# Experts of an MoE layer: gathering four experts at once and scattering in float32r parts, gates on the down product, a shorter ring

## The chip, the cores and the metric

The kernel runs on one core of a Trainium2 chip. Times are device microseconds (us) of that core. The time before is the median of three runs; the profile is of one further execution. In the text PE is TensorE, DVE VectorE, ACT ScalarE, POOL GpSimd, and SP the engine on whose queue the weights are loaded.

## The reference, cut to what matters

The reference is one layer over 256 latent tokens of width 2048: modulations, one input projection, retention and attention heads, an output projection, a norm, a hierarchical mixture of experts, a second norm. The change lies in the mixture:

```python
g_onehot = one_hot(argmax(g_logits), 4)                  # 1 of 4 groups
top_v, top_i = top_k(e_logits_of_the_group, 2)           # 2 of its 8 experts
top_w = softmax(top_v) * g_prob
for gi in range(4):                                      # 32 experts, D = 2048, hidden 512
    hid = silu(t @ w_gate[gi]) * (t @ w_up[gi])
    y = y + (hid * gate[gi]) @ w_down[gi]
```

Here t is the token after the first norm, with a shift and a scale. All arithmetic is in 32-bit floats.

## The kernel before, in words

The 32 experts are taken as 16 pairs, counted here from 0 (loop at L1093). Each expert has room for 64 tokens, so that a pair fills 128 rows. An expert's weights are 12 chunks of 1 MB, 8 for gate and up and 4 for down: 384 chunks, which SP loads in order (`stream`, L141) into a ring of 15 tiles (9 of the pool `ring`, 4 of `st`, 2 of `sa`). `expert_chunk` (L967) starts the load of the chunk 14 places ahead; the load waits until its tile is free. Two of the first chunks go to tiles that are used for other things later (`early_chunks`, L977).

For a pair the work is: one-hot matrices `oh` of which token sits in which row (L1097); the gather, `gather_some`, a product of the normalised tokens `nn` with `oh` in float32, 32 products of 128x128 in four PSUM banks, evacuated with scale and shift to `xg` by DVE (L997) and ACT (L994) in turn; gate and up of the first expert, `gate_up`, 32 products (L1013), then silu on ACT (L1016), a product on DVE (L1017), two transposes (L168) and a copy to `hT` on ACT (L1022); the down product of the first expert, four blocks of 512 columns, each 8 products (L1031) and two DVE products with modulation 5 into `Dm` (L1035); gate and up of the second expert; and then four steps, one for each block of 512 columns: the down product of the second expert and the scatter, a float32 product of `Dm` with `sT` (L1041), which DVE adds to the residual `h` (L1042). `sT` is the transpose of the one-hots times the gates, `go` (L1114). Where a row of the profile counts float32 products of PE it counts two passes for each, so 8 products of the down step stand as x16.

A scheduler places the instructions of each engine in order. PE, DVE and ACT each work through theirs one after the other, so that what waits holds up all that stands behind it on that engine. After pair 4 the kernel reads from memory whether an expert has more than 64 tokens and branches (`overflow`, L1046); it has not, so the branch leads past the loop. In the first `gate_up` of pair 15 the weights of the second norm are brought to all partitions by PE (`norm2_weights`, L1086) and ACT (L1088). Before pair 0, `nn` is made by POOL (L900) for the first 128 tokens and by ACT (L898) for the others, while DVE does the router.

Of the kernel before, what the change touches and what calls it, by code (L numbers as in the profile page):

```python
# [10 lines left out]
F32 = mybir.dt.float32  # L11
# [14 lines left out]
LOOKAHEAD = 14  # L26
EARLY = (7, 14)
# [41 lines left out]
# columns of the small weights  # L69
# [51 lines left out]
def tile_kernel(ctx: ExitStack, tc, a, out):  # L121
# [28 lines left out]
    # ---------------------------------------------------------------- constants  # L150
# [26 lines left out]
    def affine(eng, hp, mean, rstd, wt, b, nbias):  # L177
        """Normalise, scale and shift, on VectorE or on GpSimd."""
# [22 lines left out]
    # ------------------------------------------------- modulations 2..5, rows of w_ada on VectorE  # L201
# [74 lines left out]
    def matmul3(p, l, rr, first=True, last=True):  # L276
        """Product of operands in two parts each, without the product of the two small ones."""
# [4 lines left out]
    # ---------------------------------------------------------------- retention heads  # L282
# [25 lines left out]
    def ret_setup():  # L308
# [23 lines left out]
        # powers of the decay for the context: column (tile, direction, head)  # L332
# [11 lines left out]
    def ret_tables(h):  # L344
        """Decay between latent tokens (a diagonal tile and both off it), and from the context."""
# [12 lines left out]
    def ret_head(h):  # L358
# [4 lines left out]
        # state left by the context, both directions  # L363
# [35 lines left out]
    def ret_norm(h0):  # L399
        """Normalise four heads."""  # L400
# [29 lines left out]
    def mla_latents():  # L430
        # normalised latents, transposed in place
# [30 lines left out]
        # rotary keys, on both halves of the partitions  # L462
# [8 lines left out]
    # ---------------------------------------------------------------- phase A  # L471
# [170 lines left out]
    with tc.tile_pool(name="ml", bufs=1) as ml, tc.tile_pool(name="ml2", bufs=2) as ml2:  # L642
        cqT, kvT, kpT = mla["cqT"], mla["kvT"], mla["kpT"]
        # rotary queries
# [8 lines left out]
        # latents in two parts; rotary keys and queries with the parts one above the other  # L653
# [23 lines left out]
        def up(g):  # L677
            """Keys, values and queries of two heads."""
# [81 lines left out]
    # ---------------------------------------------------------------- output projection, first norm  # L760
    ring = ctx.enter_context(tc.tile_pool(name="ring", bufs=9))
# [43 lines left out]
    def router_part(n, half):  # L805
        """Two blocks of 128 columns, transposed into what is no longer needed of modulation 2."""
# [76 lines left out]
    # ---------------------------------------------------------------- router  # L883
    nnp = ctx.enter_context(tc.tile_pool(name="nnp", bufs=1, side="right"))
    nn = nnp.tile([128, 2, D], F32)
    ro = ctx.enter_context(tc.tile_pool(name="ro", bufs=1))
    # 1 / deviation and -mean / deviation
    for t in range(2):
        for j, (c0, c1) in enumerate(((CUT, D), (0, CUT))):
            A.activation(nn[:, t, c0:c1], h[:, t, c0:c1], AF.Square, bias=hs[:, t, 2:3],  # L890
                         accum_out=hs[:, t, 4 + j:5 + j])
# [5 lines left out]
        if t:  # L897
            A.activation(nn[:, t], h[:, t], AF.Identity, bias=hs[:, t, 5:6], scale=hs[:, t, 4:5])  # L898
        else:
            G.tensor_scalar(nn[:, t], h[:, t], hs[:, t, 4:5], hs[:, t, 5:6], op0=OP.mult, op1=OP.add)  # L900
# [21 lines left out]
    # one more than the rank of a token among those of the same expert, 0 where it is not sent there  # L922
# [8 lines left out]
    def router_weights():  # L931
        # weights of the chosen two
# [29 lines left out]
    order = [i for i in range(last + 8) if i not in EARLY] + list(range(last + 12, last + 20))  # L962
    for n in range(4):
        order += [last + 8 + n, last + 20 + n]
    fetched, early = {}, {}

    def expert_chunk(i):  # L967
        if i in early:
            return early.pop(i)
        pos = order.index(i)  # L970
        while len(fetched) <= min(pos + LOOKAHEAD, len(order) - 1):
            j = len(fetched)
            pool = (st, sa, ring)[(j % 15 >= 4) + (j % 15 >= 6)]
# [3 lines left out]
    def early_chunks():  # L977
        """Two of the first chunks, in tiles that have another use later."""
        for i, name in zip(EARLY, ("Dm", "xg")):
            t = mo.tile([128, D], F32, name=name, **({"bufs": 1} if name == "Dm" else {}))  # L980
            SP.dma_start(t, dram2(a["wexp"], i * 128 * D, 128, D))
            early[i] = t

    def gather_some(xg, k4, oh, width):
        p = bankT()
        for j in range(4):
            for t in range(2):
                T.matmul(p[:, 128 * j:128 * j + width], nn[:, t, 128 * (k4 + j):128 * (k4 + j) + 128],  # L988
                         oh[:, t, :width], start=(t == 0), stop=(t == 1))
        for j in range(4):  # L990
            k = k4 + j
            src = p[:, 128 * j:128 * j + width]
            if j % 2:
# [6 lines left out]
    def new_xg():  # L1000
        return mo.tile([128, D], F32, name="xg").rearrange("p (k n) -> p k n", k=KB)

    def gate_up(xg, c0, src, before=None):
        """Hidden values of up to 64 tokens, transposed."""
# [12 lines left out]
        V.tensor_tensor(hid, pg[:, 256:512], hid, op=OP.mult)  # L1017
        pt = bankT()
# [6 lines left out]
    def down(hT, src, Dm, half, n):  # L1025
# [7 lines left out]
        for cg in range(2):  # L1033
            sl = slice(512 * n + 256 * cg, 512 * n + 256 * cg + 256)
            V.tensor_tensor(Dm[rows, sl], pd[64 * cg:64 * cg + 64, :256], mod5[rows, sl], op=OP.mult)  # L1035

    def scatter(Dm, sT, K, n):
        sl = slice(512 * n, 512 * n + 512)
        for t in range(2):
            p = bankA()  # L1040
            T.matmul(p, sT[:K, t, :], Dm[:K, sl], start=True, stop=True)  # L1041
            V.tensor_tensor(h[:, t, sl], p, h[:, t, sl], op=OP.add)  # L1042

    def overflow():
        v = nc.values_load(flag[0:1, 0:1], min_val=0, max_val=256)
        with tc.If(v > CAP):  # L1046
            with tc.For_i(0, E, 1) as e:
                with tc.For_i(1, S // CAP, 1) as c:
                    rc = mo.tile([128, 2, 1], F32, name="rc", bufs=1)
                    gc = mo.tile([128, 2, 1], F32, name="gc", bufs=1)  # L1050
                    V.tensor_copy(rc, rk[:, :, ds(e, 1)])
                    V.tensor_copy(gc, gt[:, :, ds(e, 1)])
                    io = mo.tile([128, 64], F32, name="io", bufs=1)
                    V.tensor_copy(io, C("iota")[:, ds(c * CAP + 1, CAP)])
                    oh = mo.tile([128, 2, 64], F32, name="ohf", bufs=1)
                    go = mo.tile([128, 2, 64], F32, name="gof", bufs=1)
# [162 lines left out]
```

## Time and profile before

| | |
|---|---|
| three runs | 1730.43, 1731.16, 1734.97 us; median 1731.16 us |
| span of the profiled execution | 1728.5 us |
| PE busy | 1595.0 us (92% of the span) |
| DVE busy | 860.4 us (50%) |
| ACT busy | 381.5 us (22%) |
| POOL busy | 115.2 us (7%) |
| first product of pair 0 to the end of the span | 718.97 to 1728.5 us |

The profiled execution has no time of its own beside its span, which lies 2.7 us under the median of the three runs. The median counts what lies around the span too.

How to read it: a busy PE of 92% says little, since the matmuls overlap. What counts in the expert stage is the distance from one pair to the next (60.34 us for most pairs), what PE does in it one after the other, and whether the loads keep pace with it.

### The profile page before, as it was taken

The page shows a single profiled execution, that of the slowest core. Times are in us where ns is not written, and L with a number is a line of the kernel's source. Part 1 is how long each engine was busy: PE and PEld are TensorE (multiplying, and loading weights), DVE is VectorE, ACT ScalarE, POOL GpSimd, SP SyncE. Part 2 cuts the span into 40 slices and gives each one's busy share as a digit, 9 for nine tenths or more (in the row PEclk, how much of TensorE's full clock was granted, in tenths as well). Part 3 has the DMA queues.
Part 4 walks back from the last instruction along what each step waited for, and adds up shares of the span by engine and source line. Part 5 has one row for each costly group of instructions (what it writes and reads, how often), then busy time and mean ns, then how long its engine had stood idle before and what let it go on. Part 6 is the DMA issues. An engine that isn't in the chain of part 4 may idle for free. (4 is left out here: it accounts for less than half of the span.)

```text
span 1728.5 us, 21531 instructions
## 1 busy us (share of the span) xinstructions
PE 1595.0 (92%) x8730; PEld 958.4 (55%) x8730; DVE 860.4 (50%) x1563; ACT 381.5 (22%) x710; POOL 115.2 (7%) x94
## 2 busy tenths in 40 slices
PE   5999999987889899599999979999999999999995
PEld 4667686866868777344454434554444454444442
DVE  6877685798798777622331321332323233232306
ACT  3323232334665433410100000110010011001010
POOL 1000000074322100200000000000000000000001
PEclk8999999999999999799999999999999999999998
DMA  7787777756554589798999998999999999999981
GB/s 317 282 330 284 304 305 282 271 206 225 187 195 168 227 301 360 297 368 347 417 419 417 417 376 332 409 420 419 415 418 420 416 418 419 418 416 417 419 303 49
DMA packets 81591, 579.36 MB, mean 335 GB/s; under 512 B 9360, under 2 KB 9808, under 8 KB 11856
## 3 DMA queue, kind: packets, MB, share of 16 engines
q1 hardware_dynamic: 81360, 577.91, 83.8%
q8 instruction: 70, 1.15, 0.3%
q14 instruction: 33, 0.27, 0.0%
q0 software_dynamic: 128, 0.03, 0.0%
HBM read 575.81 MB, written 2.10 MB: 334 GB/s over the span
## 5 line engine op out<-in xcount | busy, mean ns | idle before, releaser
L1013 PE MATMUL pA<-st,xg 128*64 128x512 f32 x2032 | 447.5, 593 | 0.1
L1013 PEld LDWEIGHTS pA<-st,xg 128*64 128x64 f32 x2032 | 144.3, 137 | 273.0 <-issue 255.1
L1031 PE MATMUL pA<-st,hT 128*64 128x256 f32 x2048 | 238.5, 383 | 4.6 <-ACT hT L1022 4.6
L1017 DVE TENSOR_TENSOR hid<-pA,hid 128x256 f32<-128x256 f32 x32 | 13.6, 425 | 420.1 <-ACT hid L1016 420.1
L1031 PEld LDWEIGHTS pA<-st,hT 128*64 128x64 f32 x2048 | 140.0, 137 | 109.1 <-issue 26.9
L584 PE MATMUL pA<-wlo,xhi 128*128 128x512 f32 (+1 forms) x480 | 188.1, 392 | 10.3 <-DVE wlo L263 10.2
L583 PE MATMUL pA<-whi,xhi 128*128 128x512 f32 (+1 forms) x480 | 185.4, 394 | 3.4 <-ACT whi L262 3.3
L262 ACT CAST whi<-st 128x1024 fp32r<-128x1024 f32 (+3 forms) x130 | 124.7, 962 | 287.0 <-PE pA L585 175.0
L1035 DVE TENSOR_TENSOR Dm<-pA,ada_acc 64x256 f32<-64x256 f32 x256 | 108.1, 422 | 160.7 <-PE pA L1031 158.3
L585 PE MATMUL pA<-whi,xlo 128*128 128x512 f32 (+1 forms) x480 | 185.8, 387 | 0.0
L239 DVE SCALAR_TENSOR_TENSOR ada_acc<-st,c,ada_acc 128x1024 f32<-128x1024 f32 x128 | 176.8, 1401 | 11.2 <-DMA st<-in_ada_dram 11.0
L263 DVE TENSOR_TENSOR wlo<-st,whi 128x1024 fp32r<-128x1024 f32 (+2 forms) x122 | 134.7, 1112 | 56.0 <-ACT whi L262 55.4
L988 PEld LDWEIGHTS pT<-oh,nn 128*128 128x128 f32 x1024 | 125.6, 196 | 38.8 <-issue 38.0
L988 PE MATMUL pT<-oh,nn 128*128 128x128 f32 x1024 | 138.5, 286 | 7.1 <-PEq L1046 5.5
L994 ACT ACTIVATE xg<-pT,modt 128x128 f32<-128x128 f32 x128 | 58.4, 458 | 332.9 <-DVE xg L997 328.7
L1041 PE MATMUL pA<-Dm,sT 128*128 128x512 f32 x256 | 121.2, 596 | 4.9 <-DVE Dm L1035 4.9
L1016 ACT ACTIVATE hid<-pA 128x256 f32<-128x256 f32 x32 | 12.3, 384 | 497.2 <-PE pA L1013 497.2
L1042 DVE TENSOR_TENSOR h<-pA,h 128x512 f32<-128x512 f32 x128 | 88.3, 690 | 57.2 <-PE pA L1041 57.2
L583 PEld LDWEIGHTS pA<-whi,xhi 128*128 128x128 f32 x480 | 90.5, 191 | 37.6 <-ACT whi L262 17.9
L584 PEld LDWEIGHTS pA<-wlo,xhi 128*128 128x128 f32 x480 | 91.8, 191 | 32.2 <-DVE wlo L263 14.5
L585 PEld LDWEIGHTS pA<-whi,xlo 128*128 128x128 f32 x480 | 92.0, 192 | 16.3
L997 DVE TENSOR_SCALAR xg<-pT,modt 128x128 f32<-128x128 f32 x128 | 52.1, 408 | 50.8 <-PE pT L988 23.1
(342 smaller groups left out, 1462.2 us busy)
## 6 DMA issues: line engine op xcount, KB each, us to landing
st<-in_wexp_dram SPq DMA_DIRECT2D x382, 1024.0 KB, 12.3
st<-in_ada_dram SPq DMA_DIRECT2D x96, 1024.0 KB, 6.8
st<-in_win_dram SPq DMA_DIRECT2D x35, 1024.0 KB, 6.8
st<-in_wo_dram SPq DMA_DIRECT2D x16, 1024.0 KB, 5.0
st<-in_wuq_dram SPq DMA_DIRECT2D x3, 1024.0 KB, 4.8
xn<-in_x_dram SPq DMA_DIRECT2D x2, 1024.0 KB, 6.5
xn<-in_ctx_dram SPq DMA_DIRECT2D x2, 1024.0 KB, 17.0
st<-in_wukv_dram SPq DMA_DIRECT2D x2, 1024.0 KB, 5.0
```

Of the source, the lines that this page charges most:

```text
L239: V.scalar_tensor_tensor(accs[m][:, sl], w[:, sl], c2[:, k, 0:1], accs[m][:, sl], op0=OP.mult, op1=OP.add)
L262: A.copy(hi, src)
L263: (eng or V).tensor_tensor(lo, src, hi, op=OP.subtract)
L583: T.matmul(banks[t][:, :wd], xh[:, sl], hi[:, kk, :wd], start=fst, stop=False)
L584: T.matmul(banks[t][:, :wd], xh[:, sl], lo[:, kk, :wd], start=False, stop=False)
L585: T.matmul(banks[t][:, :wd], xl[:, sl], hi[:, kk, :wd], start=False, stop=lst)
L988: T.matmul(p[:, 128 * j:128 * j + width], nn[:, t, 128 * (k4 + j):128 * (k4 + j) + 128], oh[:, t, :width], start=(t == 0), stop=(t == 1))
L1013: T.matmul(pg[64 * cg:64 * cg + 64], xg[:, k, c0:c0 + 64], c[:, kk, 512 * cg:512 * cg + 512], start=(k == 0), stop=(k == KB - 1))
L1031: T.matmul(pd[64 * cg:64 * cg + 64, :256], hT[:, f % 2, 64 * (f // 2):64 * (f // 2) + 64], c[:, f, 256 * cg:256 * cg + 256], start=(f == 0 ...
L1035: V.tensor_tensor(Dm[rows, sl], pd[64 * cg:64 * cg + 64, :256], mod5[rows, sl], op=OP.mult)
L1041: T.matmul(p, sT[:K, t, :], Dm[:K, sl], start=True, stop=True)
L1042: V.tensor_tensor(h[:, t, sl], p, h[:, t, sl], op=OP.add)
```

## The change

The chunk list, the number of experts in a pair and the products of gate, up and down stay. What changes:

- The gather is for four experts at a time, 256 rows, in float32r: `nn` is split into a high and a low part (a cast on ACT, L262, and a subtraction on DVE, L263), and each of the 16 blocks takes four products of 128x256. The tile `xg` is now 16 KB wide a partition and has one buffer. The plain `nn` is made by DVE alone, in four pieces.
- `gather_all` for the next four experts stands after the second `gate_up` of every odd pair, and behind the overflow branch for experts 24 to 27.
- The gates no longer stand in the one-hots: `back` makes a column of gates, `gcol`, and the DVE instruction of the down product multiplies by it as well. The transposed one-hots `sT` are float32r.
- The scatter splits `Dm` into a high and a low part, again by ACT and DVE, and takes four float32r products of 128x512 instead of two float32 ones.
- The ring pool has 6 tiles, 12 in all, the load runs 11 chunks ahead, and no chunk is loaded early elsewhere.
- The overflow branch stands after pair 5. The weights of the second norm have their own tile.

```diff
-LOOKAHEAD = 14
-EARLY = (7, 14)
+RING = 6
+LOOKAHEAD = 5 + RING
...
-            A.activation(nn[:, t], h[:, t], AF.Identity, bias=hs[:, t, 5:6], scale=hs[:, t, 4:5])
-            G.tensor_scalar(nn[:, t], h[:, t], hs[:, t, 4:5], hs[:, t, 5:6], op0=OP.mult, op1=OP.add)
+        for c0 in (0, D // 2):
+            cs = slice(c0, c0 + D // 2)
+            V.tensor_scalar(nnf[t][:, cs], h[:, t, cs], hs[:, t, 4:5], hs[:, t, 5:6], op0=OP.mult, op1=OP.add)
+            hi_lo(nnh[0][:, t, cs], nnh[1][:, t, cs], nnf[t][:, cs])
...
+    def new_xg():
+        return mo.tile([128, KB, 256], F32, name="xg", bufs=1)
+    def gather_two(xg, k2, oh, width):
+        p = bankT()
+        for j in range(2):
+            for i in range(4):
+                T.matmul(p[:, 256 * j:256 * j + width], nnh[i % 2][:, i // 2, ks], oh[:, i // 2, :width],
+                         start=(i == 0), stop=(i == 3))
...
-            V.tensor_tensor(Dm[rows, sl], pd[64 * cg:64 * cg + 64, :256], mod5[rows, sl], op=OP.mult)
+            V.scalar_tensor_tensor(Dm[rows, sl], pd[64 * cg:64 * cg + 64, :256], gcol[rows, half:half + 1],
+                                   mod5[rows, sl], op0=OP.mult, op1=OP.mult)
...
     def scatter(Dm, sT, K, n):
         sl = slice(512 * n, 512 * n + 512)
+        hl = [mo.tile([128, 512], F32R, name=f"D{j}") for j in range(2)]
+        hi_lo(hl[0][:K], hl[1][:K], Dm[:K, sl])
         for t in range(2):
             p = bankA()
-            T.matmul(p, sT[:K, t, :], Dm[:K, sl], start=True, stop=True)
+            for j in range(2):
+                T.matmul(p, sT[:K, t, :], hl[j][:K], start=(j == 0), stop=(j == 1))
             V.tensor_tensor(h[:, t, sl], p, h[:, t, sl], op=OP.add)
...
+            hid = gate_up(xg, 128 * pq + 64, src[1])
+            if pq and not final and q != 2:
+                xg = gather_all(q + 1, lambda: hT.append(flip_hid(hid)))
+            else:
+                hT.append(flip_hid(hid))
...
-        if pr == 4:
-            overflow()
+            if pr == 5:
+                overflow()
+                xg = gather_all(q + 1)
```

Where the instructions come to stand shows the order in which the scheduler left them. First PE in the four steps at the end of a pair, before (pair 3; L1031 is the down product, L988 the gather of the next pair, L1041 the scatter):

```order
L168 MATMUL pT<-ct,hid 128x128 x2
L988 MATMUL pT<-oh,nn 128x128 x3
L1031 MATMUL pA<-st,hT 64x256 x8
L988 MATMUL pT<-oh,nn 128x128 x5
L1041 MATMUL pA<-Dm,sT 128x512 x2
L1031 MATMUL pA<-st,hT 64x256 x8
L988 MATMUL pT<-oh,nn 128x128 x5
L1041 MATMUL pA<-Dm,sT 128x512 x2
```

and now, in pair 4, which has no gather (L1053 is the down product, L1067 the scatter; D_7217 is the high part of a block and D_7218 its low part, D_7242 and D_7243 those of the next block):

```order
L1053 MATMUL pA<-st,hT 64x256 x8
L1042 MATMUL pT<-gt,oh 128x2 x2
L1067 MATMUL pA<-D_7217,sT 128x512 x2
L1053 MATMUL pA<-st,hT 64x256
L1067 MATMUL pA<-D_7218,sT 128x512 x2
L1053 MATMUL pA<-st,hT 64x256 x7
L1067 MATMUL pA<-D_7242,sT 128x512 x2
L1053 MATMUL pA<-st,hT 64x256
L1067 MATMUL pA<-D_7243,sT 128x512 x2
```

The five gather products that stood between a down product and its scatter are gone, and between the products of the high and of the low part stands one product of the next block.

Next PE behind the second `gate_up` of pair 3, which now holds the gather of experts 8 to 11 (L991; a number behind a name tells buffers apart, so pT_6231 to pT_6264 are four of the eight banks' worth of results; 8 products go to each):

```order
L991 MATMUL pT_6231<-oh_6172,nn0_5490 128x256
...
L1053 MATMUL pA_6277<-st_6081,hT_6218 64x256
L991 MATMUL pT_6242<-oh_6172,nn0_5490 128x256
...
L991 MATMUL pT_6253<-oh_6172,nn0_5490 128x256
...
L1053 MATMUL pA_6277<-st_6081,hT_6218 64x256 x2
L991 MATMUL pT_6264<-oh_6172,nn0_5490 128x256
...
L1053 MATMUL pA_6277<-st_6081,hT_6218 64x256 x5
L168 MATMUL pT_6427<-ct_69,oh_6172 128x128 x2
L1042 MATMUL pT_6432<-gt_4698,oh_6172 128x2 x2
L1067 MATMUL pA_6292<-D0_6288,sT_6055 128x512
```

Six of the eight banks' worth now stand between the second `gate_up` and the first scatter, in and around the first down product; two more stand ahead of that `gate_up`.

Last DVE in the router, just ahead of pair 0 (`nnf` is the plain `nn`, nn_5491 its low part, `sel` the choice of experts, L916 to L926 the router's steps):

```order
L903 TENSOR_SCALAR nnf<-h,hs 128x1024
L263 TENSOR_TENSOR nn_5491<-nnf,nn_5490 128x1024 x3
L903 TENSOR_SCALAR nnf<-h,hs 128x1024
L917 MAX_INDEX gi<-gm,L 128x8
L916 MAX gm<-L 128x8
L941 TENSOR_SCALAR w<-gm 128x1
L918 CAST gf<-gi 128x8
```

All four L903 and all four L263 stand ahead of `sel`; none of them was on DVE before.

## Rows read from the trace of the kernel before

**Rows 1.** Windows: start:end, length, busy (instructions) by engine; clock; DMA share, GB/s.

```profile
1163.64:1223.98 60.34, 58.15 (x343) 28.54 (x343) 17.95 (x44) 5.18 (x12) 0.00 (x0) 1.00 1.01 419
968.35:1038.27 69.92, 56.68 (x311) 26.28 (x310) 16.69 (x40) 3.80 (x9) 0.00 (x0) 0.98 0.94 386
1038.27:1103.31 65.04, 62.92 (x376) 32.36 (x375) 19.54 (x47) 6.55 (x15) 0.00 (x0) 1.00 0.89 366
1646.32:1728.50 82.18, 62.60 (x343) 28.74 (x342) 31.69 (x55) 10.86 (x20) 5.87 (x4) 0.91 0.44 164
```

**Rows 2.** SP's waits: us in total, times, longest.

```profile
SPq L141 <- PE pA L1013: 421.6, 236, 21.1
```

**Rows 3.** Chain of waits in pair 7: start, us, what.

```profile
1202.41 1.88 PE pA L1031 x16
1204.29 1.31 PE pT L988 x10
1205.60 1.72 PE pA L1041 x4
...
1222.04 2.01 PE pT L988 x18
```

**Rows 4.** Timeline, a step of pair 4: start, us, engine, what, idle before.

```profile
1006.96 1.95 PE L1031 MATMUL pA<-st,hT 128*64 128x256 f32 x16 [0.52 <-ACT hT L1022]
...
1008.95 0.86 DVE L1035 TENSOR_TENSOR Dm<-pA,ada_acc 64x256 f32<-64x256 f32 x2 [3.00 <-PE pA L1031]
...
1009.86 1.98 PE L1041 MATMUL pA<-Dm,sT 128*128 128x512 f32 x4 [0.96 <-DVE Dm L1035]
...
1011.78 1.95 PE L1031 MATMUL pA<-st,hT 128*64 128x256 f32 x16
```

**Rows 5.** Groups of instructions: busy us, mean ns of one, idle before.

```profile
L262 ACT CAST whi<-st 128x512 fp32r<-128x512 f32 x18 | 11.1, 619 | 14.1 <-PE pA L585 14.1
L263 DVE TENSOR_TENSOR wlo<-st,whi 128x512 fp32r<-128x512 f32 x18 | 11.8, 676 | 2.0 <-ACT whi L262 1.9
L428 DVE SCALAR_TENSOR_TENSOR mix<-pT,sm,mix 128x256 fp32r<-128x256 f32 x8 | 3.5, 471 | 0.2 <-ACT mix L427 0.2
L545 ACT ACTIVATE xf<-pT,modc 128x256 f32<-128x256 f32 x32 | 16.4, 561 | 6.0 <-DVE modc L526 3.2 <-DVE xlo L547 2.5 <-PE pT L168 0.4
L1041 PE MATMUL pA<-Dm,sT 128*128 128x512 f32 x256 | 121.2, 596 | 4.9 <-DVE Dm L1035 4.9
L988 PE MATMUL pT<-oh,nn 128*128 128x128 f32 x1024 | 138.5, 286 | 7.1 <-PEq L1046 5.5 <-issue 1.1 <-DVE oh L1097 0.5
L263 DVE TENSOR_TENSOR wlo<-st,whi 128x1024 fp32r<-128x1024 f32 x95 | 116.2, 1229 | 53.9 <-ACT whi L262 53.5
L199 DVE TENSOR_SCALAR xn<-xn,bnm,bnr 128x2048 f32<-128x2048 f32 x4 | 5.3, 1334 | 0.0
```

**Rows 6.** Timeline, float32r products of 128x512, then of 128x256.

```profile
585.42 0.39 PE L834 MATMUL pA<-whi,mix 128*128 128x512 f32 x1
585.65 0.39 PE L835 MATMUL pA<-wlo,mix 128*128 128x512 f32 x1
...
503.70 0.28 PE L278 MATMUL pA<-whi,kv 128*128 128x256 f32 x1
503.82 0.28 PE L279 MATMUL pA<-cq,whi 128*128 128x256 f32 x1
```

**Rows 7.** Timeline, the start of the expert stage.

```profile
707.05 1.91 DVE L896 SCALAR_TENSOR_TENSOR L<-L,hs,rc 128x40 f32<-128x40 f32 x1
...
715.60 1.86 DVE L1114 TENSOR_SCALAR go<-ct,rk,gt 128x64 f32<-128x64 f32 x8
...
718.97 7.09 PE L1013 MATMUL pA<-st,xg 128*64 128x512 f32 x32
```

**Rows 8.** Timeline, behind the branch, and norm weights in pair 15.

```profile
1031.87 4.20 PE L988 MATMUL pT<-oh,nn 128*128 128x128 f32 x23 [5.49 <-PEq L1046]
...
1650.27 1.16 PE L1086 MATMUL pT<-ct,sm 128*128 128x128 f32 x8
```

More of the change, by code (lines that the diff above doesn't have):

```diff
@@ L961, in tile_kernel @@
     last = (E - 2) * 12
-    order = [i for i in range(last + 8) if i not in EARLY] + list(range(last + 12, last + 20))
+    order = list(range(last + 8)) + list(range(last + 12, last + 20))
     for n in range(4):
         order += [last + 8 + n, last + 20 + n]
-    fetched, early = {}, {}
+    fetched = {}
     def expert_chunk(i):
-        if i in early:
-            return early.pop(i)
         pos = order.index(i)
@@ L1017, in gate_up, with flip_hid @@
         V.tensor_tensor(hid, pg[:, 256:512], hid, op=OP.mult)
+        return hid
+    def flip_hid(hid):
         pt = bankT()
@@ L1023, in gate_up, with places, back, down @@
         return hT
-    def down(hT, src, Dm, half, n):
+    def places(oh, rank, c0, width, first):
+        for t in range(2):
+            V.tensor_scalar(oh[:, t, c0:c0 + width], first, rank[:, t], None, op0=OP.is_equal)
+    def back(oh, gates, width):
+        p = bankT()
+        for t in range(2):
+            transpose(p[:width, 128 * t:128 * t + 128], oh[:, t].bitcast(F32))
+        sT = mo.tile([128, 2, 128], F32R, name="sT")
+        V.tensor_copy(sT[:width].rearrange("p t n -> p (t n)"), p[:width, :256])
+        q = bankT()
+        for t in range(2):
+            T.matmul(q[:width, 0:2], oh[:, t].bitcast(F32), gates[:, t], start=(t == 0), stop=(t == 1))
+        gcol = mo.tile([128, 2], F32, name="gcol")
+        V.tensor_copy(gcol[:width], q[:width, 0:2])
+        return sT, gcol
+    def down(hT, src, Dm, gcol, half, n):
         rows = slice(64 * half, 64 * half + 64)
@@ L1140, in tile_kernel, with new_places, gather_all @@
-    lnw, lnb = nn[:, 0], nn[:, 1]
+    def new_places(q):
+        oh = mo.tile([128, 2, 256], F32R, name="oh")
+        for s in range(4):
+            places(oh, rk[:, :, 4 * q + s:4 * q + s + 1], 64 * s, 64, C("iota")[:, 1:65])
+        return oh
+    def gather_all(q, between=None):
+        ohs[q] = new_places(q)
+        xg = new_xg()
+        for k2 in range(0, KB, 2):
+            gather_two(xg, k2, ohs[q], 256)
+            if between and k2 == 4:
+                between()
+        return xg
@@ new lines, in tile_kernel @@
+    ohs = {0: new_places(0)}
+    xg = new_xg()
+    for q in range(E // 4):
+        for pq in range(2):
+            pr = 2 * q + pq
+            final = pr == E // 2 - 1
+            src = [lambda j, e=2 * pr + s: expert_chunk(e * 12 + j) for s in range(2)]
+            if final:
+                nns.close()
+                lnwb = ctx.enter_context(tc.tile_pool(name="lnp", bufs=1, side="right")).tile([128, 2, D], F32, name="lnwb")
+            if pr:
+                hid = gate_up(xg, 128 * pq, src[0], norm2_weights if final else None)
+            else:
+                hid = gate_up(xg, 0, src[0], lambda kc: gather_two(xg, 2 * kc, ohs[0], 256))
+                router_weights()
+                ada_finish(5)
+            sT, gcol = back(ohs[q][:, :, 128 * pq:128 * pq + 128], gt[:, :, 2 * pr:2 * pr + 2], 128)
+            hT = [flip_hid(hid)]
+            Dm = new_Dm()
+            if not final:
+                for n in range(4):
+                    down(hT[0], src[0], Dm, gcol, 0, n)
+            hid = gate_up(xg, 128 * pq + 64, src[1])
+            if pq and not final and q != 2:
+                xg = gather_all(q + 1, lambda: hT.append(flip_hid(hid)))
+            else:
+                hT.append(flip_hid(hid))
+            for n in range(5):
+                if n < 4 and final:
+                    down(hT[0], src[0], Dm, gcol, 0, n)
+                if n:
+                    scatter(Dm, sT, 128, n - 1)
+                    if final:
+                        for t in range(2):
+                            V.bn_stats(st2[:, t, n - 1], h[:, t, 512 * n - 512:512 * n])
+                if n < 4:
+                    down(hT[1], src[1], Dm, gcol, 1, n)
+            if pr == 5:
+                overflow()
+                xg = gather_all(q + 1)
```

119 lines of the change are left out of this document (33 added, 86 removed).

## The prediction

> **What bounds the kernel now.** I read the windows first, one from each pair's first gate product to the next one's, because the expert stage is most of the span and its pairs repeat. Twelve of the pairs 1 to 14 take 60.34 us like the one shown, with PE at full clock and the DMA share at 1.01, 419 GB/s [rows 1]. A pair is 24 chunks of 1,048,576 bytes; at 419 GB/s that is 60.1 us. So two things are nearly level: PE's program of a pair, 60.34, and the loads, 60.1. The reader is to see that shortening PE's program alone can give back at most 0.3 us a pair, but lengthening it costs in full. Pairs 4 and 5, on either side of the branch, are 69.92 and 65.04, together 14.3 over two ordinary ones, with the DMA share down to 0.94 and 0.89 [rows 1]: there the loads lose time as well. Then the queue's waits: SP waits mostly for the gate products to free tiles [rows 2], so a tile that PE frees late starts a load late.
>
> Third, the chain of waits inside a pair: nearly all of it is PE. A step at its end is down 1.88, gather 1.31, scatter 1.72, 4.91 from step to step, and behind the last scatter stand 2.01 of gather [rows 3]. Fourth, the timeline of pair 4, which has no gather in its steps: PE ends the down product at 1008.91, idles 0.96 for the two DVE products (0.86) that make `Dm`, and comes to the next down product 4.82 after this one began [rows 4]. So in other pairs the gather in a step fills a wait that would be there anyway: 1.31 of PE work costs 0.09. That is the key to the change.
>
> **Part by part.** The sum is made against the profiled span, 1728.5, which lies 2.7 below the median.
>
> *PE's own work.* The scatter has 256 float32 passes [rows 5], 0.43 apart (1.72 for four, rows 3); it gets 256 float32r products of 128x512 at 0.23 (585.42 to 585.65) [rows 6]: about 52 us less. The gather has 1024 passes [rows 5], 0.112 apart (2.01 for 18, rows 3), and gets 512 at 0.12 [rows 6]: some 55 less. What matters is what waits are bared.
>
> *A step.* The first scatter product now needs the high part. Behind the last down product come two DVE products, 0.86 [rows 4] (0.94 by the nearest instruction with a scalar and two operands, 471 ns, rows 5; I take 0.9), the cast on ACT, 0.62 [rows 5], and handovers of some 0.1: PE waits 1.6, where nothing stands in front of it to fill the time. Then two products of the high part, 0.45, one of the next down product, 0.23, beside which DVE subtracts (0.68, rows 5), two of the low part, 0.45, and seven down products, 14 passes of 0.117, 1.64. A change from scatter to down costs 0.2 (1009.86 to 1011.78 is 1.92 for four passes of 0.43, rows 4), and there are two now: 0.4. In all 4.77, against 4.91 with gather and 4.82 without. The 0.8 that the scatter saves in a step is spent on the cast and on the second change. Were the changes free it would be 4.4; were the subtraction 0.1 late each time, 4.9.
>
> *Pairs without a gather* (2, 4, 8, 10, 12, 14). Gone are the 2.01 behind the last scatter; the four steps give 0.5 or nothing. The other gather products lay in waits. I take 60.34 - 1.8 = 58.5 each. Six of them: -11.
>
> *Pairs with a gather* (1, 3, 7, 9, 11, 13). `xg` has one buffer, so none of the eight evacuation rounds can start until the second gate_up has read the old one. Two banks' worth, 16 products, stand ahead; 16 x 0.12 is 1.9, with changes of shape about 2.0. The other six, 48 products, stand behind it, ahead of the first scatter. A bank is refilled after DVE has emptied half of it (0.47 to 0.54: between the two-operand row of that size, 471 ns, and the ACT row), then ACT the other half (0.56) [rows 5], then PE takes 8 x 0.115 = 0.92. Over two banks that is a round every 1.1 to 1.4. From the end of gate_up to the last down product I count 1.2 for the first bank, six rounds of 1.2, five down products left over 1.2 and transposes 0.4, 10.0, where a pair without a gather has 1.9 for `hid` and 1.9 of down, 3.8; a part of the first wait overlaps, and I take 6.5 to 6.9. So 58.5 + 2.0 + 6.7 = 67.2, six times 6.9 more: +41. If every round were at 0.92 it would be 5 less for each pair, if at 1.4, 1.2 more.
>
> The Trainium skill ("TensorE: Matmul & The Clock Gate", section Part 3, Packing small matmuls) says that a weight load overlaps running matmuls only when it goes to other row groups of the array. By that every gather product, which fills all of them, would pay its load too, some 0.11 by the page's rate for 128 columns (an estimate), and eight gathers of 64 would take about 55 us more in all, a time near 1,815. The trace disagrees: float32r products of 128x256 on the whole array start 0.12 apart [rows 6]. I go by the trace.
>
> *Overflow pairs.* Pair 5 has no gather of its own; behind the branch PE idles about 5.5 as before [rows 8], and then the whole gather stands open, eight rounds of 1.2 with little to cover them. I take 15.5 above two pairs of 58.5, 132.5 for pairs 5 and 6. Before, pairs 4, 5 and 6 were 195.3; the six ordinary pairs counted above hold pair 4. Pairs 1 to 14 together: 12 x 60.34 + 69.92 + 65.04 = 859.0 before, 6 x 58.5 + 6 x 67.2 + 132.5 = 886.7 now, +28.
>
> *The start.* DVE gets four plain pieces of 128x1024 (half of 1334 ns each, 2.7) and four subtractions of 1.23, 4.9 [rows 5], ahead of the choice of experts. It loses the 1.86 of `go`, and most of the 1.91 that an instruction of only 40 columns took beside POOL's `nn` [rows 7], of which I take 1.7 as stall, and gets a few more one-hots, 0.6. That makes +5: the first gate product at 724 instead of 718.97. The casts on ACT run beside it. In pair 0 products of 256 columns between the chunks change shape more often: +1.5, between 0 and +4.
>
> *The end.* In pair 15 the eight blocks of norm weights, 1.16 each with 0.07 of overlap [rows 8], leave its first gate_up and go to pair 14, where the bared waits take them: -8.7. The steps there have two down products and the longer wait: +2.7. Together -6.
>
> *Nothing.* The shorter ring: a pair uses its 20 gate and first down chunks some 5 ahead of an even supply of one per 2.5 us, and twelve tiles hold that; the mean of pairs 1 to 14 comes to 63.3 (886.7 / 14), longer than 60.1 of loads. That cover goes if PE's program becomes the shorter one (second rival). The gate column: a product of two columns and one copy, in waits.
>
> Sum: +5 + 1.5 + 28 - 6 = +28.5, a span of 1757, and with 2.7 a time of 1760.
>
> **Rivals.**
> *Faster: the loads bind.* If PE fills the new waits (the first scatter product does not wait for the whole cast, or rounds run at PE's pace), the mean pair drops under 60.1 and the loads set it: 16 x 0.27 = 4 less, the branch's 14.3 mostly hidden by loads that go on (12 less), end -6, start +5: 1714. For it: 107 us less PE work and twelve pairs already level with the loads. Against it: the 0.96 wait of pair 4, which nothing filled although down products without a wait of their own stood next in line [rows 4]. It decides if the new waits of a pair stay under 6.4: PE's 60.34 less 107 / 16 is 53.7, and the loads take 60.1.
> *No change.* The changes between scatter and down cost nothing where no wait follows, steps take 4.4 (0.37 x 4 x 15, 22 less), and rounds 1.0 instead of 1.2 (six rounds in six pairs, 7 less): 1731. For it: in pair 4 the second change is not shown [rows 4]. Against it: the 0.2 after every scatter that is.
> *Slower still.* The evacuations hold each other up. Each takes 0.1 more than the rows say, and the float32r products between other shapes run at 0.15: rounds of 1.5 instead of 1.2 and 0.3 in each step cost 6 x 2 + 15 x 0.8 + 4 = 28 more: 1788.
>
> **How the numbers follow.** Forecast 0.70, slower still 0.12, faster 0.13, no change 0.05. About 0.3%, 5 us, is what a measurement of this kernel can tell from no change. Slower by over 0.3%: 0.82; within: 0.05; faster: 0.13. The range of the forecast alone is 1738 to 1778: steps at 4.4 take 22 off at most, and rounds at 1.4 with steps at 4.9 add some 15. To leave out no more than 2 in 10 it is widened to 1728 to 1785.
>
> **What would show it.** In the profile after: PE busy about 100 us lower at a longer span; PE waiting for the high part on ACT 1.5 to 1.7 four times a pair; steps of 4.7 to 4.9; pairs without a gather at 58 to 59 and with one at 66 to 68; a DMA share under 1 in the mean; the first gate product near 724; no norm weights in pair 15. I am wrong if steps come under 4.4, if pairs with a gather take under 63, or if a pair is 60 with the DMA share at 1.0 throughout.

## The result and the profile after

The changed kernel takes 1855.94 us (median of 4 runs, 1850.86 to 1860.96) beside 1733.07 for the kernel before in the same comparison (4 runs): a ratio of 1.0704, 95% interval 1.0672 to 1.0735. It is slower, as forecast, but by 123 us where 29 were forecast. The profiled execution spans 1858.6 us.

The first view is again the windows, one from each pair's first gate product to the next one's: pair 6 (behind the branch), pair 7 (with a gather), pair 8 (without) and the end. The columns are those of [rows 1].

```profile
1156.47:1227.20 70.73, 61.95 (x335) 29.34 (x334) 21.25 (x47) 7.93 (x15) 0.00 (x0) 0.95 0.86 346
1227.20:1302.87 75.67, 66.56 (x347) 31.49 (x346) 21.21 (x41) 8.49 (x16) 0.00 (x0) 0.93 0.83 333
1302.87:1367.50 64.63, 55.40 (x283) 22.85 (x282) 18.35 (x41) 3.98 (x8) 0.00 (x0) 0.95 0.94 384
1782.00:1858.60 76.60, 51.81 (x283) 21.99 (x282) 35.17 (x59) 7.16 (x13) 5.95 (x4) 0.87 0.54 215
```

A pair with a gather takes 75.7 instead of 60.34, one without 64.6. The clock column, 1.00 in the ordinary pairs before, is 0.93 to 0.95, and the loads, which ran at 419 GB/s before, run at 333 to 384. The start costs 5.0 (the first gate product comes at 724.01 instead of 718.97), and the end gives back 5.6 (76.60 instead of 82.18). So the loss lies in the pairs.

Next who waited for whom: PE's longest wait over the whole span, and then SP's two longest (us in total, times, longest).

```profile
PE pA L1067 <- ACT D L262: 96.3, 60, 2.4
...
SPq L141 <- PE pA L1053: 467.7, 119, 12.2
SPq L141 <- PE pA L1013: 428.7, 247, 20.1
```

PE waits 96.3 us for the high part that ACT casts, 60 times; before, its waits for `Dm` were 4.9 in all [rows 5]. SP waits for PE to free tiles, as before [rows 2], and not for its own transfers: the loads follow PE.

Where the time goes inside a step is in the timeline of PE at the end of pair 6 (start, us, what, idle before it); the counterpart of before is [rows 4].

```profile
1206.52 0.74 PE L1067 MATMUL pA<-D,sT 128*128 128x512 f32 x2 [1.20 <-ACT D L262]
1207.19 0.90 PE L1053 MATMUL pA<-st,hT 128*64 128x256 f32 x2
1208.02 1.22 PE L1067 MATMUL pA<-D,sT 128*128 128x512 f32 x2
1209.17 2.76 PE L1053 MATMUL pA<-st,hT 128*64 128x256 f32 x14
1213.65 0.74 PE L1067 MATMUL pA<-D,sT 128*128 128x512 f32 x2 [1.73 <-ACT D L262]
1214.32 0.65 PE L1053 MATMUL pA<-st,hT 128*64 128x256 f32 x2
1214.89 0.73 PE L1067 MATMUL pA<-D,sT 128*128 128x512 f32 x2
1215.56 1.94 PE L1053 MATMUL pA<-st,hT 128*64 128x256 f32 x14
1219.30 0.74 PE L1067 MATMUL pA<-D,sT 128*128 128x512 f32 x2 [1.80 <-ACT D L262]
```

The same instructions stand in both steps. From 1213.65 to 1219.30 is 5.65; from 1206.52 to 1213.65 is 7.13, because the two middle groups and the 14 down passes took 0.90, 1.22 and 2.76 instead of 0.65, 0.73 and 1.94. The windows of that stretch show why (start:end, length, PE busy, granted clock, DMA share, GB/s):

```profile
1206.20:1207.90 1.70, 1.38 (x4) 0.86 1.02 424
1207.90:1209.60 1.70, 1.70 (x5) 0.50 1.02 424
1209.60:1211.30 1.70, 1.70 (x12) 0.63 1.00 414
```

The granted clock stood at 0.50, the lower of its two levels (1.2 of 2.4 GHz), in the whole of the second window and in part of the other two, with no transfer missing (the DMA share is 1.0 or more). It falls like this in every pair up to pair 12. Of the 45 distances from one step to the next in pairs 0 to 14, three in each pair, 22 are over 7; the others are 5.6 to 5.7. The costs of the instructions in the step, in the groups (busy us, mean ns of one, idle before), are those that the forecast took, but for the DVE instruction with the gate; the last line is the plain product in the kernel before:

```profile
L1057 DVE SCALAR_TENSOR_TENSOR Dm<-pA,gcol,ada_acc 64x256 f32<-64x256 f32 x256 | 123.7, 483 | 183.3 <-PE pA L1053 181.2
L262 ACT CAST D<-Dm 128x512 fp32r<-128x512 f32 x64 | 39.5, 617 | 299.8 <-DVE Dm L1057 294.1 <-PE pA L1053 5.4
...
L1035 DVE TENSOR_TENSOR Dm<-pA,ada_acc 64x256 f32<-64x256 f32 x256 | 108.1, 422 | 160.7 <-PE pA L1031 158.3
```

The instruction with the gate takes 483 ns, against 422 for the plain product that it replaces; the cast takes 617, as forecast.

### The profile page after: what moved, and what is told of

Read it like the earlier page. It is cut to its first block, busy times and chain, and to the rows that moved or that the text cites. A ratio compares the mean times of both kernels' runs of the same rounds, so it can differ in the third digit from the quotient of the medians.

```text
span 1858.6 us, 20553 instructions
## 1 busy us (share of the span) xinstructions
PE 1620.1 (87%) x8282; PEld 934.0 (50%) x8282; DVE 894.1 (48%) x1523; ACT 400.1 (22%) x713; POOL 113.9 (6%) x93
## 5 line engine op out<-in xcount | busy, mean ns | idle before, releaser
L1013 PE MATMUL pA<-st,xg 128*64 128x512 f32 x2048 | 475.1, 602 | 0.0
L1053 PE MATMUL pA<-st,hT 128*64 128x256 f32 x2048 | 301.6, 414 | 6.3 <-ACT hT L1025 6.3
L1053 PEld LDWEIGHTS pA<-st,hT 128*64 128x64 f32 x2048 | 159.1, 148 | 128.8 <-issue 53.1
L1057 DVE SCALAR_TENSOR_TENSOR Dm<-pA,gcol,ada_acc 64x256 f32<-64x256 f32 x256 | 123.7, 483 | 183.3 <-PE pA L1053 181.2
L1067 PE MATMUL pA<-D,sT 128*128 128x512 f32 x256 | 107.1, 504 | 97.0 <-ACT D L262 96.3
L262 ACT CAST whi<-st 128x1024 fp32r<-128x1024 f32 (+3 forms) x130 | 124.9, 963 | 285.5 <-PE pA L585 171.9
L263 DVE TENSOR_TENSOR wlo<-st,whi 128x1024 fp32r<-128x1024 f32 (+2 forms) x122 | 134.7, 1113 | 56.0 <-ACT whi L262 55.5
L1067 PEld LDWEIGHTS pA<-D,sT 128*128 128x128 f32 x256 | 43.0, 210 | 157.8 <-ACT D L262 119.8
L1068 DVE TENSOR_TENSOR h<-pA,h 128x512 f32<-128x512 f32 x128 | 82.5, 687 | 81.4 <-PE pA L1067 81.3
L1000 DVE TENSOR_SCALAR xg<-pT,modt 128x256 f32<-128x256 f32 x64 | 34.8, 543 | 146.9 <-PE pA L1013 78.7
L262 ACT CAST D<-Dm 128x512 fp32r<-128x512 f32 x64 | 39.5, 617 | 299.8 <-DVE Dm L1057 294.1
L991 PE MATMUL pT<-oh,nn 128*128 128x256 f32 x512 | 78.8, 302 | 17.8 <-ACT xg L997 7.5
```

The costliest lines, as they stand in the source:

```text
L991: T.matmul(p[:, 256 * j:256 * j + width], nnh[i % 2][:, i // 2, ks], oh[:, i // 2, :width], start=(i == 0), stop=(i == 3))
L1013: T.matmul(pg[64 * cg:64 * cg + 64], xg[:, k, c0:c0 + 64], c[:, kk, 512 * cg:512 * cg + 512], start=(k == 0), stop=(k == KB - 1))
L1053: T.matmul(pd[64 * cg:64 * cg + 64, :256], hT[:, f % 2, 64 * (f // 2):64 * (f // 2) + 64], c[:, f, 256 * cg:256 * cg + 256], start=(f == 0 ...
L1057: V.scalar_tensor_tensor(Dm[rows, sl], pd[64 * cg:64 * cg + 64, :256], gcol[rows, half:half + 1], mod5[rows, sl], op0=OP.mult, op1=OP.mult)
L1067: T.matmul(p, sT[:K, t, :], hl[j][:K], start=(j == 0), stop=(j == 1))
```

## The experiments

Three theories were held against each other. A: the time is lost in the steps, to the wait for two DVE products and a cast and to a clock that falls after it. B: it is lost to the ring of 12 tiles, since the DMA share is down. C: it is lost in the float32r gather. Ratios are to the kernel before, with 95% intervals.

| run | median us | ratio |
|---|---|---|
| changed kernel | 1855.94 | 1.0704 (1.0672 to 1.0735) |
| before_ring12 | 1731.22 | 0.9993 (0.9976 to 1.0009) |
| scat_f32 | 1767.46 | 1.0201 (1.0143 to 1.0259) |
| scat_copy | 1806.40 | 1.0424 (1.0399 to 1.0448) |
| scat_copy3 | 1908.24 | 1.1015 (1.0983 to 1.1046) |
| fill | 1937.60 | 1.1183 (1.1121 to 1.1244) |
| fill2 | 1819.90 | 1.0497 (1.0467 to 1.0528) |
| hi_only | 1702.12 | 0.9818 (0.9786 to 0.9849) |
| before_split | 1771.50 | 1.0218 (1.0188 to 1.0248) |
| before_lag2 | 1743.09 | 1.0052 (1.0036 to 1.0067) |
| lag2 | 1709.41 | 0.9866 (0.9792 to 0.9939) |
| lag2_again | 1704.72 | 0.9853 (0.9822 to 0.9883) |
| lag2_early | 1708.03 | 0.9857 (0.9838 to 0.9875) |

**before_ring12**: the ring alone.

```diff
-LOOKAHEAD = 14
-EARLY = (7, 14)
+LOOKAHEAD = 11
+EARLY = ()
...
-    ring = ctx.enter_context(tc.tile_pool(name="ring", bufs=9))
+    ring = ctx.enter_context(tc.tile_pool(name="ring", bufs=6))
...
-            pool = (st, sa, ring)[(j % 15 >= 4) + (j % 15 >= 6)]
+            pool = (st, sa, ring)[(j % 12 >= 4) + (j % 12 >= 6)]
...
-    early_chunks()
```

> The kernel before with the ring of 12 tiles and no chunk loaded early, nothing else. Theories A and C: PE's program of a pair is unchanged and 12 tiles hold it, so 1733 to 1742 (five chunks fewer are loaded ahead of pair 0). Theory B: 1800 or more.

Measured 1731.22, no difference. Three tiles fewer and five early chunks fewer cost nothing in the kernel before. In the changed kernel itself B falls with lag2 below: with the same ring of 12 its loads run at 419 GB/s. So the low DMA share after the change is a result, not a cause.

**scat_f32**: the scatter back in float32, all else as changed.

```diff
-        sT = mo.tile([128, 2, 128], F32R, name="sT")
+        sT = mo.tile([128, 2, 128], F32, name="sT")
...
-        hl = [mo.tile([128, 512], F32R, name=f"D{j}") for j in range(2)]
-        hi_lo(hl[0][:K], hl[1][:K], Dm[:K, sl])
         for t in range(2):
             p = bankA()
-            for j in range(2):
-                T.matmul(p, sT[:K, t, :], hl[j][:K], start=(j == 0), stop=(j == 1))
+            T.matmul(p, sT[:K, t, :], Dm[:K, sl], start=True, stop=True)
```

> The changed kernel with the scatter back as one float32 product of the unsplit block (no cast, no subtraction), the gates still on the down product, the float32r gather of four kept. Theory A: the wait in a step is that for the two DVE products alone, 1.0, the clock stays up, a step takes 4.9 instead of 5.6 to 7.3; pairs without a gather come to 59, those with one to 69, the whole to 1765 to 1785. Theories B and C: 1850, since ring and gather are the same.

Measured 1767.46. So 88 of the 123 us are the split scatter, and C falls as the main cause. Pairs with and without a gather, in this kernel's windows (columns as in [rows 1]):

```profile
1186.00:1253.79 67.79, 61.40 (x348) 29.47 (x347) 18.77 (x36) 5.97 (x12) 0.00 (x0) 1.00 0.96 395
1253.79:1312.20 58.41, 51.90 (x284) 21.76 (x283) 15.90 (x36) 1.51 (x4) 0.00 (x0) 1.00 0.97 401
```

The pairs take 67.8 and 58.4, at a clock of 1.00. The remaining 34 us over before belong to the rest of the change: the gather of four, the gate column, the start and the end. No run tells these apart.

**fill**: products put into the wait, to see whether an idle PE lowers the clock.

```diff
+FILL = 12
...
+        for i in range(FILL if fill is not None else 0):
+            T.matmul(pd[:, 256:512], fill[:, 0, 0:128], fill[:, i % 2], start=True, stop=True)
         for cg in range(2):
...
-                    down(hT[1], src[1], Dm, gcol, 1, n)
+                    down(hT[1], src[1], Dm, gcol, 1, n, ohs[q])
```

> The changed kernel with twelve more float32r products of 128x256 behind each down product of the second expert, into columns of its bank that nobody reads; they stand in the wait of 1.8 us and take 1.4. If the waits are what lowers the granted clock, it stays at 1.0 in the steps, which go from 7.1 to 5.7 where it fell, 3 us a pair: about 1805 in spite of 768 products more. If the clock falls for another reason, or costs nothing: 1856 or more. Should the DVE products wait for the added ones too, each step is 1.4 longer: 1940.

Measured 1937.60: the last case. The added products stand in the bank that DVE reads, and DVE waited for them, so the wait behind them stayed at 1.78. In the timeline of pair 7 (L1057 are the added products, which PE works at from 1314.38 to 1316.07, L1060 the two DVE products and L1070 the scatter):

```profile
1316.12 0.99 DVE L1060 SCALAR_TENSOR_TENSOR Dm<-pA,gcol,ada_acc 64x256 f32<-64x256 f32 x2 [2.44 <-PE pA L1057]
...
1317.86 0.73 PE L1070 MATMUL pA<-D,sT 128*128 128x512 f32 x2 [1.78 <-ACT D L263]
```

So the run doesn't fill the wait, but it shows what more products do that leave the wait as it is: the clock still fell, in 17 of the 45 distances between steps (8.8 to 8.9 instead of 7.3), against 22 in the changed kernel.

**fill2**: the same with a bank of its own.

```diff
+FILL = 6
...
+        return hl[0]
+
+    def fill(lhs, rhs):
+        pf = bank("G", 1)
+        for i in range(FILL):
+            T.matmul(pf[:, :rhs.shape[-1]], lhs, rhs, start=True, stop=True)
...
-                    scatter(Dm, sT, 128, n - 1)
+                    hi = scatter(Dm, sT, 128, n - 1)
...
                     down(hT[1], src[1], Dm, gcol, 1, n)
+                    if n:
+                        fill(sT[:, 0, :], hi)
```

Here `hi` is the high part of the block before.

> The changed kernel with six more float32r products of 128x512 behind the second to fourth down product of the second expert of a pair, 1.4 us in a wait of 1.8; they read the high part of the block before and write a bank that nothing else uses, so that no DVE instruction waits for them. If PE standing still in these waits is what lowers the granted clock, it stays at 1.0 in the steps behind them, which go from 7.1 to 5.7: 2 to 3 us a pair, 1810 to 1825 in spite of 288 products more. If the clock falls for another reason (the mix of float32 and float32r products), 1856 to 1870.

Measured 1819.90, within what was expected from an idle PE. The timeline of PE in this kernel's pair 7 (L1068 is the scatter, L1054 the down product, L1075 the fill), and the windows of pairs 8 and 9:

```profile
1264.07 0.73 PE L1068 MATMUL pA<-D,sT 128*128 128x512 f32 x2 [0.20 <-ACT D L263]
1264.74 0.65 PE L1054 MATMUL pA<-st,hT 128*64 128x256 f32 x2
1265.31 0.73 PE L1068 MATMUL pA<-D,sT 128*128 128x512 f32 x2
1265.97 1.94 PE L1054 MATMUL pA<-st,hT 128*64 128x256 f32 x14
1267.84 1.66 PE L1075 MATMUL pG<-D,sT 128*128 128x512 f32 x6
1269.72 0.74 PE L1068 MATMUL pA<-D,sT 128*128 128x512 f32 x2 [0.21 <-ACT D L263]
...
1276.04:1337.52 61.48, 57.02 (x301) 25.23 (x300) 18.38 (x41) 3.99 (x8) 0.00 (x0) 1.00 0.96 390
1337.52:1408.39 70.87, 66.54 (x365) 32.99 (x364) 21.16 (x41) 8.50 (x16) 0.00 (x0) 1.00 0.93 373
```

The step shown is 5.65, the clock of these pairs is 1.00, and they take 61.5 and 70.9 instead of 64.6 and 75.7. Only 3 of the 45 distances between steps are over 7, each behind the first scatter of a pair, whose wait is not filled. A kernel with more products and the same step at full clock is 36 us faster: at least that much of the loss is the clock. The added products are float32r too, so it isn't the mix of float32 and float32r that lowers it.

**scat_copy** and **scat_copy3**: the same wait without a float32r product in the scatter. ACT copies the block, in place of the cast, once or three times over.

This is scat_copy against the changed kernel; in scat_copy3 three `A.copy` stand one behind the other, the last into `dc`.

```diff
-        sT = mo.tile([128, 2, 128], F32R, name="sT")
+        sT = mo.tile([128, 2, 128], F32, name="sT")
...
-        hl = [mo.tile([128, 512], F32R, name=f"D{j}") for j in range(2)]
-        hi_lo(hl[0][:K], hl[1][:K], Dm[:K, sl])
+        dc = mo.tile([128, 512], F32, name="dc")
+        A.copy(dc[:K], Dm[:K, sl])
         for t in range(2):
             p = bankA()
-            for j in range(2):
-                T.matmul(p, sT[:K, t, :], hl[j][:K], start=(j == 0), stop=(j == 1))
+            T.matmul(p, sT[:K, t, :], dc[:K], start=True, stop=True)
```

> The changed kernel with the float32 scatter, but of a copy of the block that ACT makes (a plain float32 copy in the place of the cast; no float32r product, no subtraction in the scatter). PE's wait is then as long as with the cast, 1.7 to 1.8, without the changes between float32 and float32r. If the length of the wait is what lowers the granted clock, it falls as in the changed kernel: 0.7 a step and about 3 a pair more than with the float32 scatter alone, 1840 to 1860. If the mix of float32 and float32r products lowers it, it stays at 1.0 and only the wait counts, 64 x 0.7: 1805 to 1815.

> As the run with the float32 scatter of a copy, but with three copies on ACT one behind the other, so that PE waits 3.1 a step instead of 1.8; no float32r product in the scatter. At a clock of 1.0 that is 64 x 1.3 more than with one copy: 1885 to 1895. If standing still lowers the clock as soon as it is long enough beside the products of a step, float32 or not, it falls here in the steps, 3 or more a pair: 1925 to 1950. If only float32r products in the step make it fall, 1885 to 1895.

With one copy the time was 1806.40: the lower case. PE's waits are as long as in the changed kernel, and the clock stays up: none of the 45 distances between steps is over 5.7. This kernel's longest wait of PE, two steps of its timeline, and two windows of that stretch (start:end, length, PE busy, granted clock, DMA share, GB/s), the first mostly in a wait and the second in the scatter behind it:

```profile
PE pA L1066 <- ACT dc L1063: 94.9, 58, 1.8
...
1262.17 1.98 PE L1066 MATMUL pA<-dc,sT 128*128 128x512 f32 x4 [1.80 <-ACT dc L1063]
1264.09 1.95 PE L1053 MATMUL pA<-st,hT 128*64 128x256 f32 x16
1267.85 1.98 PE L1066 MATMUL pA<-dc,sT 128*128 128x512 f32 x4 [1.81 <-ACT dc L1063]
...
1260.00:1262.00 2.00, 0.38 (x4) 1.00 0.89 291
1262.00:1264.00 2.00, 1.83 (x4) 1.00 0.90 377
```

So a wait of 1.8 does not lower the clock by itself: my theory in that form fell. What differs is what stands between the waits, 1.92 us of float32 scatter here and 1.9 us of float32r scatter with a down product in its middle there. With three copies the time was 1908.24, between my two cases; with no float32r product in the scatter the clock then fell in some pairs and not in others. Here are two steps of pair 7, and two windows of 20 us over steps of pair 7 and of pair 8:

```profile
1306.93 3.16 PE L1053 MATMUL pA<-st,hT 128*64 128x256 f32 x16
1313.14 3.52 PE L1069 MATMUL pA<-dc,sT 128*128 128x512 f32 x4 [3.04 <-ACT dc L1066]
1316.58 1.95 PE L1053 MATMUL pA<-st,hT 128*64 128x256 f32 x16
1321.57 1.98 PE L1069 MATMUL pA<-dc,sT 128*128 128x512 f32 x4 [3.04 <-ACT dc L1066]
...
1300.00:1320.00 20.00, 13.17 (x58) 0.83 0.58 231
1380.00:1400.00 20.00, 11.50 (x54) 1.00 0.83 337
```

Four scatter passes took 3.52 behind one wait and 1.98 behind the next, and 13 of the 45 distances between steps are longer than at full clock (6.90). So float32r in the scatter is not needed for the fall, and the length of a single wait doesn't settle it. What does stays open.

**hi_only**: DVE writes the down product as float32r at once, and only that is scattered; the low part is left out.

> The changed kernel with the down product written by DVE as float32r at once and only this high part scattered (the low part, the cast and the subtraction are left out): two products a step instead of four, and a wait for the two DVE products alone. Theory A (cast, second change of shape, clock): PE waits 1.0, the clock stays up, a step takes 3.8 to 4.0, pairs without a gather 54 to 55, with one 63 to 65, less than the loads in the mean, which become the bound: 1700 to 1725. If it were the float32r products among float32 ones, or the single buffer of the gather: 1760 or more.

Measured 1702.12, as expected: without the cast the wait is 1.0 (55.0 us in 57 waits) and the loads become the bound (SP waits 394.9 us in total for its own transfers, the longest of its waits). This kernel computes less than the others and shows only where the time lies.

**before_split**: the split scatter and the gates on the down product alone, in the kernel before.

> The kernel before with the scatter in two float32r parts and the gates on the down product, its float32 gather of two experts kept (ring of 14 tiles, for room). The gather fills 0.6 to 0.9 us of each wait of 1.8, so the clock should stay at 1.0 in pairs with a gather in the steps; a step is then 5.5 to 5.7 instead of 4.9, a pair 62 to 63: 1755 to 1780. If the clock falls all the same, 1800 to 1830; if the split costs nothing when the gather stands in the wait, 1733 or less.

Measured 1771.50, as expected. A step of its pair 7 (L988 is the gather, L1059 the scatter):

```profile
1229.29 0.73 PE L1059 MATMUL pA<-D,sT 128*128 128x512 f32 x2
...
1233.06 2.05 PE L988 MATMUL pT<-oh,nn 128*128 128x128 f32 x16
1234.91 0.73 PE L1059 MATMUL pA<-D,sT 128*128 128x512 f32 x2
```

The float32 gather fills the wait, and the clock is up (one of the 45 distances between steps is over 7). A step still is 5.62 instead of 4.91, as long as with the unfilled wait (5.65): 16 gather passes stand in it where 10 stood [rows 3]. So even with the wait filled, the split with its gate column costs more than the float32 products that it saves.

**lag2**: the changed kernel with the scatter two down blocks behind.

```diff
-            for n in range(5):
-                if n < 4 and final:
-                    down(hT[0], src[0], Dm, gcol, 0, n)
-                if n:
-                    scatter(Dm, sT, 128, n - 1)
+            for n in range(6):
+                if n < 4:
+                    if final:
+                        down(hT[0], src[0], Dm, gcol, 0, n)
+                    down(hT[1], src[1], Dm, gcol, 1, n)
+                if n > 1:
+                    m = n - 2
+                    scatter(Dm, sT, 128, m)
...
-                if n < 4:
-                    down(hT[1], src[1], Dm, gcol, 1, n)
```

> The changed kernel with the scatter of a block two down blocks behind instead of one, nothing else. Theory A (the time is lost in the steps: PE waits 1.8 us for two DVE products and a cast, and its granted clock falls to half after such waits): the next down product fills the wait, PE's wait for the high part falls from 96 us to under 30, the clock stays at 1.0 in most steps, pairs lose about 10 us each and the loads become the bound: 1700 to 1740. Theory B (the time is lost to the ring of 12 tiles, the DMA share is only 0.83 on average): 1840 or more, since the ring is untouched. Theory C (the float32r gather pays its weight loads): 1840 or more as well, with pairs without a gather at 58 and those with one at 70 or more.

Measured 1709.41, and 1704.72 when run again. The end of its pair 8 in PE's timeline, SP's longest wait, and the windows of pairs 8 and 9 (columns as in [rows 1]):

```profile
1249.39 3.67 PE L1053 MATMUL pA<-st,hT 128*64 128x256 f32 x32
1252.99 1.19 PE L1067 MATMUL pA<-D,sT 128*128 128x512 f32 x4
1254.11 1.95 PE L1053 MATMUL pA<-st,hT 128*64 128x256 f32 x16
1255.99 1.44 PE L1067 MATMUL pA<-D,sT 128*128 128x512 f32 x5
1257.58 0.97 PE L1067 MATMUL pA<-D,sT 128*128 128x512 f32 x3 [0.16 <-DVE D L263]
...
SPq L141 <- DMA st<-in_wexp_dram: 515.5, 264, 3.2
...
1206.35:1259.99 53.64, 50.12 (x285) 22.25 (x285) 18.93 (x44) 3.99 (x8) 0.00 (x0) 1.00 1.01 419
1259.99:1325.71 65.72, 58.92 (x346) 28.36 (x345) 19.88 (x38) 8.50 (x16) 0.00 (x0) 1.00 1.01 419
```

The next down block stands where PE waited; only behind the last down block short waits are left, 0.16 in the lines shown and 0.78 ahead of the fourth scatter. The four scatter products come together: 1.12 from the first to the next down product, against 1.90 in the changed kernel with a down product in their middle (1282.09 to 1283.99 in its pair 7). SP now waits for its transfers first, and the loads run at 419 GB/s through pairs with and without a gather: they are the bound.

**before_lag2**: the lag without the change.

> The kernel before with the scatter two down blocks behind, nothing else of the change. If the gain of the changed kernel with that lag comes from the lag alone, 1705 to 1715. If it needs PE's shorter program too (the gather and the scatter in float32r, about 107 us less): the waits of before were filled already, pairs stay at 60 with the loads, 1724 to 1735.

Measured 1743.09, slower by 0.5%, outside both of my cases: pairs take 61.5, although PE waits nowhere in the steps. The gather products no longer fill waits, for there are none, and behind the last scatter stand 38 passes of them, where 18 stood before [rows 3]:

```profile
1287.48 2.62 PE L988 MATMUL pT<-oh,nn 128*128 128x128 f32 x22
...
1291.03 2.05 PE L988 MATMUL pT<-oh,nn 128*128 128x128 f32 x16
```

So the lag alone gives nothing; the gain of lag2 needs PE's shorter program.

**lag2_early** and **lag2_again**:

> The changed kernel with the scatter two blocks behind, and one of the first chunks loaded ahead into the tile of the down product, as the kernel before did. With the loads as the bound from pair 1 on, a chunk more ahead of pair 0 is 2.5 less: 1703 to 1709. If the start of pair 0 decides instead, the same as without it.

> The changed kernel with the scatter two blocks behind once more, timed in three rounds beside the kernel before: 1703 to 1713, faster than before by 1.2 to 1.7%.

1708.03 and 1704.72: the chunk loaded ahead gives nothing that shows. The version to keep is lag2, faster than the kernel before by 1.5% (ratio 0.9853, 0.9822 to 0.9883).

## Why the prediction was wrong, point by point

- *The start*, +5 and the first gate product at 724: it came at 724.01. Right.
- *The end*, -6: 82.18 became 76.60. Right.
- *Pairs with a gather* 67.2, *without* 58.5, *overflow pairs* 132.5: measured 75.7, 64.6 and 146.2. With the scatter left in float32 they are 67.8, 58.4 and 133.8. So a gather's surplus over a pair without one was priced nearly rightly, 9.4 against 8.7, though the 6.5 to 6.9 in it do not follow from the 10.0 less 3.8 that stand before them. That this kernel's 1767 lies so near the forecast of 1760 is in part luck: its float32 step is 4.95, near the 4.77 that I forecast for the split one.
- *Pair 0*, +1.5: 76.5 instead of 68.4, +8.1. With the float32 scatter it is 70.9, so 5.6 of the miss is again the steps.
- *A step*, 4.77: this is the step that failed. At full clock it is 5.65, 0.88 more. The three groups from the first scatter product to the run of 14 down passes take 0.67, 0.57 and 0.67 (from 1213.65, 1214.32 and 1214.89), 1.91 in all, where I had 0.45 + 0.23 + 0.45 and 0.4 for two changes, 1.53. Beyond the products themselves that is 0.22 for each change from scatter to down, as [rows 4] show, and 0.34 for the one from down to scatter, which I did not charge: it was hidden behind a wait there. The rest, 3.74 against 3.24, is the two DVE products (0.98 instead of 0.90), the handovers, and some 0.3 from the pace of the last down passes to the start of DVE. 0.88 in the four steps of 15 pairs is some 53 us.
- *The clock*, which I had at 1.0 throughout. It isn't in my sum at all, and in the pairs shown it costs 3.1 without a gather (64.6 against 61.5 in fill2) and 4.8 with one (75.7 against 70.9). [Rows 1] did show a clock of 0.98 around the branch and 0.91 at the end, and I read past it. With the 36 us by which fill2 is faster, the step and the clock make 89 of the 96 us by which the forecast missed. The Trainium skill ("TensorE: Matmul & The Clock Gate", section A second HAM failure mode: psum-queue depth-cycling) tells of a kernel in which short idle stretches between groups of matmuls come often enough to make the clock go back and forth. The trace agrees for the changed kernel, 0.50 in stretches behind waits of 1.8; the run with one copy, with the same waits and a clock of 1.00, shows that short waits alone don't suffice.
- *The faster rival* did not happen, but its mechanism is the one that lag2 brings about: with new waits under 6.4 a pair the loads bind. It gave 1714; lag2 takes 1705 to 1709.
- *The float32r gather's weight loads*: not paid, as I took it. 16 gather products take 2.07 in the changed kernel, 0.13 apiece. The 1815 that the prediction works out by the rule of the Trainium skill ("TensorE: Matmul & The Clock Gate", section Part 3, Packing small matmuls) lies nearer to the measured time than my 1760, but by chance: the same gather stands in the runs at 1767 and 1705.
- *Slips in the sums.* In the rival *slower still*, 0.3 in each step is 1.2 a pair and not 0.8, which gives 1794 and not 1788; in the range, 1760 and the 15 added are 1775 and not 1778. Neither comes near 1856.

The loss of 123 us in pieces, each by a difference of two kernels: the gather of four, start and end 34 (scat_f32 less before); the wait for ACT's piece 39 (scat_copy less scat_f32); the split and the clock together 50 (changed kernel less scat_copy). Of these 50, filling three of the four waits of a pair gives back 36. That is a lower bound for the clock: in the profiles fill2 is 43 shorter in pairs 1 to 14, but 5 longer in pair 15, where the added products stand as well. At full clock a step is 5.65 in the changed kernel and 5.68 in scat_copy, so beside a plain copy the split itself costs next to nothing, and nearly all of the 50 is clock.

## What to carry to other kernels

A wait between two engines is free only as long as something stands in it. When a change takes away the filler and lengthens the chain at the same time, price the whole chain, every change of tile shape in both directions, and the clock; then look for independent work with which to fill it, here the next down block, by letting the consumer run one block later. Faster products gave nothing here until that was done, and 1.5% after.

## What the runs showed of the hardware that was not expected

- Added matmuls can make a kernel faster: six in each of three waits of 1.8 us a pair took 36 us off the whole, because the granted clock fell to 0.50 in 3 of 45 steps instead of 22.
- Waits of 1.8 us lowered the clock in about half of the steps (22 of 45) beside a float32r scatter broken by a down product, and in none beside a float32 scatter; waits of 3.04 beside a float32 scatter lowered it in 13 of 45.
- Four float32r products of 128x512 take 1.12 to the next down product when they stand together, and 1.90 with one float32 product of another shape in their middle, whose own two passes are 0.23.
